# Conditions of the modulation in PSUM, half of the modulated tiles by rows on TensorE, and the first norm's roots in banks of their own

## The chip, the cores and the metric

The kernel runs on one core of one Trainium2 chip. The metric is the device time of one execution in microseconds (us). The engines are named as in the profile: PE (TensorE, matrix products), DVE (VectorE), ACT (ScalarE), POOL (GpSimd) and SP (SyncE, which issues the loads named here).

## The reference

Two layers work on a stream `x` of 1024 latent tokens by 1024 channels. Both are modulated by a conditioning vector `c`; the 256 context tokens `ctx` of the even layer are modulated by another one, `c_ctx`:

```python
sc, scc = silu(c), silu(c_ctx)
shift, scale, gate = split(sc @ mod_w[l] + mod_b[l], 3)       # 1024 -> 3 x 1024
hx = rmsnorm(x, norm_g[l]) * (1 + scale) + shift
shift_c, scale_c, _ = split(scc @ mod_w[l] + mod_b[l], 3)     # even layer only
hc = rmsnorm(ctx, norm_g[l]) * (1 + scale_c) + shift_c
```

The even layer projects `hx` and `hc` (`va, vg, ga, xb, gb`), runs a convolution branch and a bidirectional recurrence, and projects back. The odd layer projects, pools over windows, mixes inside groups with `w_grp`, gates and projects back. The whole runs in float32.

## The kernel before, in words

Channels lie on the 128 partitions and tokens along the free dimension, so `x` is eight tiles `x_0..x_7` of 128x1024 (`KT` = 8). Wide products are made of three matmuls on split operands (high by high, high by low, low by high); `split` lets ACT cast the high half (L95) and another engine subtract the low half (L96).

The change lies in the first stage, which ends with the first matmul of `project_xb(0)` (L125). Four kinds of work run side by side there:

- **The first norm of x.** ACT squares each `x` tile; POOL adds up the squares of the left half of the tokens, DVE those of the right half (L290). `rstd_cols` turns each sum into reciprocal roots: four small matmuls add over the partitions (L187), ACT takes the root (L188), DVE the reciprocal (L189) and a diagonal tile `dg_x` (L191), and one more matmul (L194; an fp32 matmul, which the trace shows as two passes) spreads the roots over all partitions. Sums and spread roots of one half share one two-bank PSUM tile, `wide(...)`.
- **The modulation vectors of layer 0, in two ways.** `modulation(k)` loads two 128x1024 tiles of `mod_w` (shift and scale of channel tile k) and multiplies each on DVE with `cL` and with `cC`, which are SiLU(c) and SiLU(c_ctx) spread over all partitions, and adds up along the row (L206; output `junk`): four big DVE instructions for each k. `mod_row(j)` does the last `KR` tiles of shift (j = 0) or scale (j = 1) on PE: the two conditions as columns (`ccv`) against pieces of `mod_w` (L313), giving two rows; ACT copies the rows (L316), small matmuls turn them into columns (`modt`, L319), and DVE adds the bias into `m0` (L321). Before, tiles 0 to 5 (`KD` = 6) go by DVE and two by rows.
- **`modulate(k)`** scales `x_k` by the roots and by `a0` (L329, two halves), ACT adds the shift and casts the high half `h0h_k` (L332), and DVE makes the low half `h0l_k` (L333). These are what `project_xb(0)` multiplies.
- **Two of the four folds of the odd layer's weights**, `fold(0)` and `fold(1)`: `w_grp` times `wu` on PE (L243 to L245), 24 matmuls for each of four pieces, with `gh`/`gl` the split group matrix (ACT and DVE, L95 and L96) and `wh_wu`/`wl_wu` the split weights (ACT and POOL). They fill PE in the stage.

The small PSUM tiles (`psum`, tag "mm") come from a pool of four banks, the wide ones from two pairs of banks, "cv" and "xb". The program is built with `schedule_with_timeline_sim=True`: a scheduler sets the order of each engine's instructions from its own estimates when the program is built, and each engine then works its list in that order. `load` puts the loads of the stage behind one another on SP's queue. After the stage, PE goes on with the projections.

Of the kernel before, what the change touches and what calls it, by code (L numbers as in the profile page):

```python
# [9 lines left out]
F32 = mybir.dt.float32  # L10
F32R = mybir.dt.float32r
AF = mybir.ActivationFunctionType
# [3 lines left out]
P = 128  # L16
# [3 lines left out]
D = 1024  # L20
KT = D // P
H = 512
HALF = (slice(0, H), slice(H, S))
# [20 lines left out]
O_FG = O_OS + 2 * KT  # L44
N_SM = O_FG + KT

KD = 6
KR = KT - KD
KW = 4 // ((KR + 1) // 2)

# [5 lines left out]
def body(ctx, tc, xT, ctxT, cc, ccol, modT, modW, win, gw, wout, wu, grp, wg, wo1, small, edge, ident, outT):  # L56
    nc = tc.nc
# [17 lines left out]
    def dtile(name, dt=F32):  # L75
        return dpool.tile([P, S], dt, tag="d", name=name)
# [4 lines left out]
    def ttile(name):  # L81
        return tpool.tile([P, H], F32, tag="t", name=name)

    def atile(name):
        return apool.tile([P, NR * PW], F32, tag="acc", name=name)

    def psum(name):
        return pm.tile([P, H], F32, tag="mm", name=name)


    def wide(name, n):
        return pc.tile([P, S], F32, tag=("cv", "xb")[n % 2], name=name)
# [8 lines left out]
    def load(out, src):  # L101
        with ExitStack() as lctx:
            if chain[0] is not None:
                lctx.enter_context(tc.issue_after(chain[0].ins))
            d = nc.sync.dma_start(out, src)
            if chain[0] is not None:
                chain[0] = d
# [27 lines left out]
    def col(o, n=1):  # L135
        return sm[:, o : o + n]

    ones = base.tile([P, P], F32, name="ones")
# [39 lines left out]
        nc.vector.reciprocal(acc, rt[:, :n])  # L178


    def rstd_cols(acc, name, idD, rpool, wn):
        n = acc.shape[-1]
        nt = n // P
        ps = wide(f"ms_{name}", wn)
        r = rpool.tile([P, H // P], F32, tag="rc", name=f"rc_{name}")[:, :nt]
        for c in range(nt):
            nc.tensor.matmul(ps[:, c : c + 1], acc[:, c * P : (c + 1) * P], ones[:, 0:1], start=True, stop=True)  # L187
        nc.scalar.activation(r, ps[:, :nt], AF.Sqrt, bias=eps_r)  # L188
        nc.vector.reciprocal(r, r)  # L189
        t = ttile(f"dg_{name}")[:, :n]  # L190
        nc.vector.tensor_tensor(out=t.rearrange("p (c t) -> p c t", t=P),  # L191
                                in0=idD.unsqueeze(1).to_broadcast([P, nt, P]),
                                in1=r.unsqueeze(2).to_broadcast([P, nt, P]), op=mult)
        nc.tensor.matmul(ps[:, H : H + n], ones, t, start=True, stop=True)  # L194
        return ps[:, H : H + n]

    m0 = base.tile([P, 2, 3 * KT], F32, name="m0")
# [4 lines left out]
    def mod_tile(t, l, m, raw, vecs, junk):  # L204
        for i, vec in enumerate(vecs):
            nc.vector.scalar_tensor_tensor(out=junk, in0=raw, scalar=1.0, in1=vec,  # L206
                                           op0=mult, op1=mult, accum_out=t[:, i, m : m + 1])
        n = len(vecs)
        v = t[:, :n, m]
        nc.vector.tensor_tensor(out=v, in0=v, in1=col(O_MB + l * 3 * KT + m).to_broadcast([P, n]), op=add)  # L210

    def mod_scale(t, a, l, k):
        n = t.shape[1]
        nc.vector.scalar_tensor_tensor(out=a[:, :, k], in0=t[:, :, KT + k], scalar=1.0,
                                       in1=col(O_NG + l * KT + k).to_broadcast([P, n]), op0=add, op1=mult)
# [38 lines left out]
    cpool = tc.alloc_tile_pool(name="cpool", bufs=1)  # L254
    cth = [cpool.tile([P, D], F32R, name=f"cth{i}") for i in range(2)]
    ctl = [cpool.tile([P, D], F32R, name=f"ctl{i}") for i in range(2)]
    cL = cpool.tile([P, D], F32, name="cL")
    hh, hl, ch, cl = [], [], [], []
    with ExitStack() as sctx:
        fpool = sctx.enter_context(tc.tile_pool(name="fpool", bufs=6))  # L260
        gpool = sctx.enter_context(tc.tile_pool(name="gpool", bufs=4))
        spool = sctx.enter_context(tc.tile_pool(name="spool", bufs=1))
# [9 lines left out]
        def fold_some(n):  # L272
            for _ in range(n):
                next(folds, None)

        cC = spool.tile([P, D], F32, name="cC")
        cx = [spool.tile([P, D], F32, name=f"cx_{i}") for i in range(2)]


# [1 line left out]
        acc = [atile("ssq0"), atile("ssq1")]  # L281
# [12 lines left out]
        def modulation(k):  # L294
            for m in (k, KT + k):
                raw = dtile(f"mod0_{m}")
                load(raw, modT[0, m])
                mod_tile(m0, 0, m, raw, (cL, cC), junk)
            mod_scale(m0, a0, 0, k)
# [3 lines left out]
        idx = spool.tile([P, P], F32, name="idx")  # L303
        ccv = spool.tile([P, KT, 2], F32, name="ccv")

        def mod_row(j):
# [11 lines left out]
            for e in range(KR):  # L318
                nc.tensor.matmul(pst[:, :, e], row[:, e * P : (e + 1) * P], idx[:2, :2], start=True, stop=True)  # L319
            ms = slice(j * KT + KD, (j + 1) * KT)  # L320
            nc.vector.scalar_tensor_tensor(out=m0[:, :, ms], in0=pst, scalar=1.0 / D,  # L321
# [35 lines left out]
        nc.scalar.activation(ccv, ccv, AF.Silu)  # L357
        load(idx, ident)
        for i, t in enumerate((cL, cC)):
            ps = wide(f"c_{i}", i)  # L360
            for h in range(2):
                nc.tensor.matmul(ps[:, HALF[h]], ones[:1], cx[i][:1, HALF[h]], start=True, stop=True)
            nc.scalar.activation(t, ps, AF.Silu, scale=float(D))
        def ctx_load(i):
            load(cx[i].rearrange("p (k n) -> p k n", n=C), ctxT[4 * i : 4 * i + 4].rearrange("k p n -> p k n"))
            for q4 in range(4):
# [23 lines left out]
        modulation(1)  # L390
        x_load(7)
        modulation(2)
        rx = [rstd_cols(acc[h][:, :H], f"x{h}", idx, spool, h) for h in range(2)]
        mod_row(1)
        mod_row(0)
        fold_some(2)
        for k in range(KD, KT):
            mod_scale(m0, a0, 0, k)
        modulation(4)
        fold_some(1)  # L400
        modulate(0)
        modulation(3)
        modulation(5)
        modulate(1)
        modulate(2)
        modulate(3)
# [14 lines left out]
    with ExitStack() as actx:  # L421
# [6 lines left out]
        def ltile(name, dt=F32):  # L428
            return lpool.tile([P, E], dt, tag="l", name=name)

        def recurrence(j, uc, gates):
            rs, ius, ats = gates[0::2], gates[1::2], []
            for d in range(2):
                cd = d * KT + j
                at = ltile(f"a{j}_{d}")
                ats.append(at)
                nc.scalar.activation(at, rs[d], AF.Exp, scale=cneg[:, cd : cd + 1])

                th = nc.scalar.activation(rs[d], rs[d], AF.Tanh, scale=chalf[:, cd : cd + 1])
                nc.gpsimd.tensor_tensor(out=ius[d], in0=ius[d], in1=uc, op=mult)  # L440
            for d in range(2):
                r, iu, at = rs[d], ius[d], ats[d]
                with tc.issue_after(th.ins):
                    nc.scalar.activation(r, r, AF.Sqrt, bias=tiny)  # L444
                nc.gpsimd.tensor_tensor(out=iu, in0=iu, in1=r, op=mult)  # L445
                nc.vector.scalar_tensor_tensor(out=iu, in0=at, scalar=1.0, in1=iu, op0=add, op1=mult)  # L446
                if d == 0:
                    ctx_, lat = slice(0, C), slice(C, E)
                    first = iu[:, C - 1 : C]
                else:  # L450
                    ctx_, lat = slice(C - 1, None, -1), slice(E - 1, C - 1, -1)
                    first = iu[:, 0:1]
                nc.vector.tensor_tensor_scan(out=iu[:, ctx_], data0=at[:, ctx_], data1=iu[:, ctx_],
                                             initial=0.0, op0=mult, op1=add)
                nc.vector.tensor_tensor_scan(out=iu[:, lat], data0=at[:, lat], data1=iu[:, lat],  # L455
                                             initial=first, op0=mult, op1=add)
            hs = ius[0]
            nc.gpsimd.tensor_tensor(out=hs[:, C:], in0=hs[:, C:], in1=ius[1][:, C:], op=add)
            nc.sync.dma_start(yb_raw[j], hs[:, C:])

            m = 2 * KT + j
            raw = ltile(f"mod0_{m}")
            nc.sync.dma_start(raw[:, :D], modT[0, m])
            mod_tile(m0, 0, m, raw[:, :D], (cL,), raw[:, :D])


        state = None
# [11 lines left out]
        for j in range(KT):  # L479
            uc = utile(f"uc{j}")  # L480

            for src, dst in zip(xb, (uc[:, :C], uc[:, C:])):
                n = src.shape[-1]
# [11 lines left out]
            for h in range(2):  # L495
                ps = psum(f"vg{j}_{h}")
                mm3(ps, w, (hh, hl), HALF[h])
                t = ttile(f"sg{j}_{h}")
# [5 lines left out]
            for h in range(2):  # L504
                ps = psum(f"va{j}_{h}")
# [9 lines left out]
            for d in range(2):  # L515
                for gi, ob in ((0, O_BR), (1, O_BI)):
                    kc = slice((2 * gi + d) * P, (2 * gi + d + 1) * P)
                    t = ltile(f"g{j}_{d}_{gi}")
                    for a, n in ((0, C), (C, H), (C + H, H)):
                        ps = psum(f"g{j}_{d}_{gi}_{a}")  # L520
# [139 lines left out]
    for j in range(KT):  # L660
        w = wload(win[4 * KT + j], f"gb{j}", nc.gpsimd)
        th, tl = d2tile(f"ybh{j}", F32R), d2tile(f"ybl{j}", F32R)
        for h in range(2):
            ps = psum(f"gb{j}_{h}")
# [48 lines left out]
    for h in range(2):  # L713
        ps = wide(f"mu{h}", h)[:, :H]
# [15 lines left out]
    for m in range(KT):  # L730
        w = wload(wout[m, 1], f"wob{m}", nc.gpsimd)
        for h in range(2):
            ps = psum(f"wob{m}_{h}")
            mm3(ps, w, (bh, bl), HALF[h])
            t = vtile(f"xp{m}_{h}")
# [36 lines left out]
    for i in range(KH):  # L772
        for j in (i, KH + i):
            w = wload(win[2 * KT + j], f"ga{j}", nc.gpsimd)
            for h in range(2):
                ps = psum(f"ga{j}_{h}")
# [63 lines left out]
    idD = cH[:, :P]  # L840
# [54 lines left out]
    for i in range(KH):  # L895
# [3 lines left out]
        t = block_sums(b11, b12, b21, b22, ttile(f"xt3_{i}"), nc.vector)  # L899
# [105 lines left out]
    for m in range(0, NK, 2):  # L1005
# [38 lines left out]
        elif m <= KT:  # L1044
            n = 2 * KT + m - 2
            for q in range(2):
                raw = dtile(f"mod1_{n + q}")
# [183 lines left out]
    m = KT - 4  # L1231
# [56 lines left out]
def layout(i):  # L1288
# [43 lines left out]
    for g, w in enumerate(WINDOWS):  # L1332
        for t in range(w // 2):
            edge[g, t] = w / (t + w // 2)
        for q in range(w // 2 - 1):
# [8 lines left out]
        "modT": f(mw.transpose(0, 2, 1).reshape(2, 3 * KT, P, D)),  # L1344
        "modW": f(mw[0].reshape(KT // KW, KW, P, 3, D)[:, :, :, :2, KD * P :].transpose(3, 0, 2, 1, 4)
                  .reshape(2, KT // KW, P, KW * KR * P)),
# [27 lines left out]
```

## Time and profile before

| | us |
|---|---|
| runs | 1391.06, 1392.81, 1392.95; median 1392.81 |
| profiled execution, time | 1389.0 |
| profiled execution, span of the instructions | 1387.1 |
| busy: PE / DVE / ACT / POOL | 1297.7 / 1172.6 / 655.7 / 401.7 |

The profiled execution is 3.8 us below the median of the runs, and 1.9 us of its time lie around the span. The mean granted PE clock is 0.972 of full speed. PE is busy 94% of the span and DVE 85%, but the shares are means over stages; the first stage is some 92 us of the 1387.1, and its rows decide what a change in it is worth.

### The profile page before, as it was taken

The numbers are of one execution on the slowest core, as the hardware profiler recorded it, in microseconds if no ns is written. First come the engines' busy times: TensorE is split into PE (matmuls) and PEld (weight loads), VectorE is DVE, ScalarE is ACT, GpSimd is POOL, SyncE is SP. The second block draws the span as 40 slices with busy tenths as digits, with TensorE's granted clock in tenths as the row PEclk, the third lists the DMA queues.
The fourth block names the chain that finished last, engine by engine and source line by source line (L and its number), as shares of the span: only waits on it lengthen the run. The fifth ranks groups of instructions, "written<-read, shape, count | busy, mean of one in ns | idle before, by whom it ended". The sixth has DMA issues, their size and how long they took to land.

```text
span 1387.1 us, 15661 instructions
## 1 busy us (share of the span) xinstructions
PE 1297.7 (94%) x5664; PEld 1051.2 (76%) x5664; DVE 1172.6 (85%) x1563; ACT 655.7 (47%) x928; POOL 401.7 (29%) x198
## 2 busy tenths in 40 slices
PE   7889989997998798999999899999999999999896
PEld 4468777786777686888888788778888888777685
DVE  7984898799888989999678874999999986886775
ACT  6352754763764672412633544754333334633442
POOL 5173626745645664542521004100000000000002
PEclk9999999999999999999999999999999999999998
DMA  9741111111211122344254636523334324757623
GB/s 352 279 137 39 38 61 53 65 58 62 68 38 69 61 76 99 107 144 151 99 188 156 212 121 205 155 88 130 134 132 144 115 94 150 253 197 266 217 107 121
DMA packets 82865, 181.79 MB, mean 131 GB/s; under 512 B 7778, under 2 KB 27618, under 8 KB 82788
## 3 DMA queue, kind: packets, MB, share of 16 engines
q1 hardware_dynamic: 74340, 176.60, 37.3%
q10 hardware_dynamic: 8448, 4.20, 1.0%
q8 instruction: 44, 0.72, 0.2%
q14 instruction: 33, 0.27, 0.1%
HBM read 136.72 MB, written 44.04 MB: 130 GB/s over the span
## 4 chain that ended last, share of the span: by engine, by line
PE 57%; DVE 24%; ACT 6%; issue 5%; DMA 4%; POOL 3%; SPq 0%; POOLq 0%; DVEq 0%; ACTq 0%
DVE conv L688 6%; DVE g L455 2%; PE wob L126 2%; PE wob L125 2%; PE wob L127 2%; PE ga L125 2%; PE ga L126 2%; PE ga L127 2%; DVE junk L206 1%; PE fold L245 1%; PE fold L244 1%; PE fold L243 1%; DVE ws L928 1%; DVE mod L206 1%; PE vg L125 1%
## 5 line engine op out<-in xcount | busy, mean ns | idle before, releaser
L688 DVE SCALAR_TENSOR_TENSOR conv<-u,sm,conv 128x1009 f32<-128x1009 f32 (+14 forms) x240 | 301.1, 1274 | 21.6 <-ACT conv L681 18.4
L1194 POOL TENSOR_TENSOR o<-x,rr 128x256 f32<-128x256 f32 (+1 forms) x9 | 8.0, 925 | 459.1 <-ACT rr L1182 456.2
L96 POOL TENSOR_TENSOR wl_wu<-wr_wu,wh_wu 128x1024 fp32r<-128x1024 f32 x16 | 38.7, 2421 | 153.1 <-ACT wh_wu L95 147.4
L521 PE MATMUL g<-uh,wh_gw 128*128 128x512 f32 (+1 forms) x96 | 40.9, 426 | 27.8 <-ACT g L524 16.7
L524 ACT ACTIVATE g<-g,sm 128x512 f32<-128x512 f32 (+1 forms) x96 | 54.0, 622 | 18.8 <-PE g L523 12.2
L125 PE MATMUL gb<-h0h,wh_gb 128*128 128x512 f32 x128 | 51.7, 404 | 5.6 <-ACT sb L669 5.6
L243 PE MATMUL fold<-gh,wh_wu 128*128 128x512 f32 x128 | 52.6, 412 | 4.6 <-ACT wh_wu L95 4.6
L244 PE MATMUL fold<-gl,wh_wu 128*128 128x512 f32 x128 | 51.7, 404 | 3.7 <-DVE gl L96 3.7
L446 DVE SCALAR_TENSOR_TENSOR g<-a,g 128x1280 f32<-128x1280 f32 x16 | 36.4, 2273 | 20.6 <-POOL g L445 20.6
L245 PE MATMUL fold<-gh,wl_wu 128*128 128x512 f32 x128 | 51.2, 409 | 2.7 <-POOL wl_wu L96 2.7
L445 POOL TENSOR_TENSOR g<-g,g 128x1280 f32<-128x1280 f32 x16 | 50.6, 3180 | 9.8 <-ACT g L444 9.8
L440 POOL TENSOR_TENSOR g<-g,uc 128x1280 f32<-128x1280 f32 x16 | 47.3, 2956 | 21.1 <-ACT g L524 19.4
L126 PE MATMUL gb<-h0l,wh_gb 128*128 128x512 f32 x128 | 51.4, 402 | 0.0
L127 PE MATMUL va<-h0h,wl_va 128*128 128x512 f32 x128 | 49.6, 391 | 2.0 <-POOL wl_va L96 2.0
L95 ACT CAST wq_wo<-wr_wo 128x512 fp32r<-128x512 f32 x48 | 28.8, 619 | 47.4 <-DMA wr_wo<-wo 13.8
L127 PE MATMUL gb<-h0h,wl_gb 128*128 128x512 f32 x128 | 51.1, 400 | 0.0
L126 PE MATMUL wob<-ybl,wh_wob 128*128 128x512 f32 x128 | 50.3, 394 | 0.0
L127 PE MATMUL ga<-h0h,wl_ga 128*128 128x512 f32 x128 | 50.2, 392 | 0.0
L127 PE MATMUL wob<-ybh,wl_wob 128*128 128x512 f32 x128 | 50.0, 393 | 0.0
L125 PE MATMUL xb<-h0h,wh_xb 128*128 128x512 f32 x128 | 49.9, 390 | 0.0
L125 PE MATMUL wob<-ybh,wh_wob 128*128 128x512 f32 x128 | 49.9, 394 | 0.0
L126 PE MATMUL xb<-h0l,wh_xb 128*128 128x512 f32 x128 | 49.9, 390 | 0.0
(549 smaller groups left out, 4360.4 us busy)
## 6 DMA issues: line engine op xcount, KB each, us to landing
mod<-modT SPq DMA_DIRECT2D x28, 512.0 KB, 3.8
wr_wu<-wu SPq DMA_DIRECT2D x16, 512.0 KB, 4.1
x_part<-xp SPq DMA_DIRECT2D x32, 256.0 KB, 3.4
mod<-modT SPq DMA_DIRECT2D x32, 256.0 KB, 3.2
wr_v<-wfold SPq DMA_DIRECT2D x16, 512.0 KB, 4.1
wr_g<-wg SPq DMA_DIRECT2D x16, 512.0 KB, 4.2
wr_wo<-wo SPq DMA_DIRECT2D x16, 512.0 KB, 4.3
yr_t<-y_t SPq DMA_DIRECT2D x16, 512.0 KB, 5.5
```

Source lines behind the costliest of these rows:

```text
L96: eng.tensor_tensor(out=lo, in0=src, in1=hi.bitcast(F32), op=sub))
L125: nc.tensor.matmul(ps, hi[:, kc], xh[k][:, cols], start=(k == 0), stop=False)
L126: nc.tensor.matmul(ps, hi[:, kc], xl[k][:, cols], start=False, stop=False)
L127: nc.tensor.matmul(ps, lo[:, kc], xh[k][:, cols], start=False, stop=(k == ks - 1))
L243: nc.tensor.matmul(ps, wh[:, kc], gh[i], start=(i == 0), stop=False)
L244: nc.tensor.matmul(ps, wh[:, kc], gl[i], start=False, stop=False)
L245: nc.tensor.matmul(ps, wl[:, kc], gh[i], start=False, stop=(i == 3))
L440: nc.gpsimd.tensor_tensor(out=ius[d], in0=ius[d], in1=uc, op=mult)
L445: nc.gpsimd.tensor_tensor(out=iu, in0=iu, in1=r, op=mult)
L521: nc.tensor.matmul(ps[:, :n], gwh[:, kc], uh[:, a : a + n], start=True, stop=False)
L524: nc.scalar.activation(t[:, a : a + n], ps[:, :n], AF.Sigmoid, bias=col(ob + d * KT + j))
L688: nc.vector.scalar_tensor_tensor(out=acp[:, a:b], in0=us[j][:, a + o : b + o], scalar=col(O_CONVW + 31 * j + k), in1=acp[:, a:b], op0=mult ...
```

## The change

1. `KD` goes from 6 to 4. Tiles 4 and 5 leave `modulation` and join 6 and 7 in `mod_row`; the eight L206 instructions of `modulation(4)` and `modulation(5)` go. Each `mod_row` still makes eight fp32 matmuls, now 512 columns wide instead of 256, from four loads of 512 KB instead of two, and turns four tiles into columns instead of two. The sum of bytes is the same: sixteen tiles of 512 KB.
2. `cL` and `cC` are no longer SBUF tiles. The product that spreads them stays in its wide PSUM tile, SiLU works in place, and L206 reads the PSUM tile. For the gates, which are made later in the recurrence, ACT copies `cL` to an SBUF tile `cS`.
3. The wide pairs are thus taken, and `rstd_cols` of x uses two "mm" banks for each half, `ms_x` for the sums and `root_x` for the spread roots. The two roots hold two of the four banks until `x_7` is scaled.

```diff
-KD = 6
+KD = 4
...
-    def rstd_cols(acc, name, idD, rpool, wn):
+    def rstd_cols(acc, name, idD, rpool, wn=None):
...
-        ps = wide(f"ms_{name}", wn)
+        if wn is None:
+            ps, root = psum(f"ms_{name}"), psum(f"root_{name}")
+        else:
+            ps = wide(f"ms_{name}", wn)
+            root = ps[:, H : H + n]
...
-        nc.tensor.matmul(ps[:, H : H + n], ones, t, start=True, stop=True)
-        return ps[:, H : H + n]
+        nc.tensor.matmul(root, ones, t, start=True, stop=True)
+        return root
...
-    cL = cpool.tile([P, D], F32, name="cL")
+    cS = cpool.tile([P, D], F32, name="cS")
...
-        cC = spool.tile([P, D], F32, name="cC")
+        cL, cC = wide("cL", 0), wide("cC", 1)
...
-            ps = wide(f"c_{i}", i)
             for h in range(2):
-                nc.tensor.matmul(ps[:, HALF[h]], ones[:1], cx[i][:1, HALF[h]], start=True, stop=True)
-            nc.scalar.activation(t, ps, AF.Silu, scale=float(D))
+                nc.tensor.matmul(t[:, HALF[h]], ones[:1], cx[i][:1, HALF[h]], start=True, stop=True)
+            nc.scalar.activation(t, t, AF.Silu, scale=float(D))
+        nc.scalar.copy(cS, cL)
...
-        rx = [rstd_cols(acc[h][:, :H], f"x{h}", idx, spool, h) for h in range(2)]
+        rx = [rstd_cols(acc[h][:, :H], f"x{h}", idx, spool) for h in range(2)]
...
-        modulation(4)
         fold_some(1)
         modulate(0)
         modulation(3)
-        modulation(5)
...
-            mod_tile(m0, 0, m, raw[:, :D], (cL,), raw[:, :D])
+            mod_tile(m0, 0, m, raw[:, :D], (cS,), raw[:, :D])
```

The scheduler orders the instructions anew. In the rows below a line number, the operation, and output and inputs stand; a trailing number of a tile only tells one use from another. First PE before, from the sums of the first norm to the first matmul of `fold(0)`'s last piece:

```order
L187 MATMUL ms_x0_422<-ones_119,ssq0_184 128x1 x4
L187 MATMUL ms_x1_433<-ones_119,ssq1_185 128x1 x4
L313 MATMUL modr_1_444<-modw_1_0_445,ccv_189 2x256 x4
L194 MATMUL ms_x0_422<-dg_x0_430,ones_119 128x512
L313 MATMUL modr_1_444<-modw_1_1_451,ccv_189 2x256 x4
L194 MATMUL ms_x1_433<-dg_x1_441,ones_119 128x512
L319 MATMUL modt_1_459<-idx_188,modrow_1_457 128x2 x2
...
L319 MATMUL modt_0_478<-idx_188,modrow_0_476 128x2 x2
L243 MATMUL fold_0_3_0_488<-gh_0_0_205,wh_wu_0_3_484 128x512
```

Here `modr_1` is cut in two and lies between the small products of the norm, and `modr_0` follows `modt_1`.

And PE after, at the same place (line numbers are 4 higher there):

```order
L191 MATMUL ms_x0_422<-ones_119,ssq0_185 128x1 x4
L198 MATMUL root_x0_423<-dg_x0_431,ones_119 128x512
L191 MATMUL ms_x1_434<-ones_119,ssq1_186 128x1 x4
L198 MATMUL root_x1_435<-dg_x1_443,ones_119 128x512
L317 MATMUL modr_1_446<-modw_1_0_447,ccv_190 2x512 x2
...
L317 MATMUL modr_1_446<-modw_1_3_459,ccv_190 2x512 x2
L323 MATMUL modt_1_465<-idx_189,modrow_1_463 128x2 x4
L317 MATMUL modr_0_471<-modw_0_0_472,ccv_190 2x512 x2
...
L317 MATMUL modr_0_471<-modw_0_3_484,ccv_190 2x512 x2
L323 MATMUL modt_0_490<-idx_189,modrow_0_488 128x2 x4
L247 MATMUL fold_0_3_0_502<-gh_0_0_205,wh_wu_0_3_498 128x512
```

Now all four products of the norm come first, and both `mod_row`s follow, ahead of the fold.

DVE before, from the bias of the last rows (`modt_0`) to the low halves `gl_1_0` and `gl_1_1` of the second fold's group matrix, on which nearly all of `fold(1)` rests:

```order
L321 SCALAR_TENSOR_TENSOR m0_160<-modt_0_478,sm_115 128x2x2
L333 SCALAR_TENSOR_TENSOR h0l_2_620<-x_2_276,m0_160,h0h_2_619 128x1024
L210 TENSOR_TENSOR m0_160<-m0_160,sm_115 128x2
L206 SCALAR_TENSOR_TENSOR junk_187,m0_160<-mod0_12_539,cL_171 128x1024
L206 SCALAR_TENSOR_TENSOR junk_187,m0_160<-mod0_12_539,cC_181 128x1024
L96 TENSOR_TENSOR gl_1_0_523<-graw_1_0_520,gh_1_0_522 128x1024
...
L96 TENSOR_TENSOR gl_1_1_529<-graw_1_1_526,gh_1_1_528 128x1024
```

The low half `gl_1_0` comes four instructions after the bias of the last rows (one of them two columns wide).

DVE after, the same stretch and the few instructions ahead of it:

```order
L210 SCALAR_TENSOR_TENSOR junk_188,m0_160<-mod0_11_599,cC_182 128x1024
L214 TENSOR_TENSOR m0_160<-m0_160,sm_115 128x2
L218 SCALAR_TENSOR_TENSOR a0_161<-m0_160,sm_115 128x2
L325 SCALAR_TENSOR_TENSOR m0_160<-modt_0_490,sm_115 128x2x4
L333 SCALAR_TENSOR_TENSOR x_3_284<-x_3_284,a0_161,root_x0_423 128x512
...
L333 SCALAR_TENSOR_TENSOR x_7_403<-x_7_403,a0_161,root_x1_435 128x512
L337 SCALAR_TENSOR_TENSOR h0l_3_620<-x_3_284,m0_160,h0h_3_619 128x1024
L337 SCALAR_TENSOR_TENSOR h0l_4_626<-x_4_368,m0_160,h0h_4_625 128x1024
L96 TENSOR_TENSOR gl_1_0_537<-graw_1_0_534,gh_1_0_536 128x1024
L337 SCALAR_TENSOR_TENSOR h0l_5_632<-x_5_376,m0_160,h0h_5_631 128x1024
L96 TENSOR_TENSOR gl_1_1_543<-graw_1_1_540,gh_1_1_542 128x1024
```

Between the instruction that takes `modt_0` from PE and `gl_1_0` there stood one `h0l` and two L206; now ten scalings of `x_3` to `x_7` (five tiles, two halves) and two `h0l` stand there, and `gl_1_1` follows one `h0l` later.

## Prediction

> **What bounds the kernel now.** I read first the busy time in stretches of the first stage, then the chain that ended last, then the engines' own rows. In the stretches the columns are the busy us (and instructions) of PE, PE's weight load, DVE, ACT and POOL, then the granted PE clock, the DMA share and GB/s:
>
> ```profile
> core 0: us, PE busy (x) PEld busy (x) DVE busy (x) ACT busy (x) POOL busy (x), PEclk, DMA share, GB/s
> 26.00:53.00 27.00, 23.68 (x102) 14.13 (x102) 26.49 (x41) 12.19 (x20) 12.09 (x7) 0.94 1.02 385
> 53.00:92.00 39.00, 30.66 (x122) 23.55 (x122) 38.79 (x52) 20.35 (x31) 21.54 (x12) 0.96 0.50 155
> 92.00:143.00 51.00, 51.00 (x250) 43.10 (x249) 26.56 (x26) 14.81 (x17) 22.01 (x16) 1.00 0.17 54
> ```
>
> Until 92 us DVE has hardly a gap (65.28 of 66 us), and PE idles 11.7 us; from 92 us on it is PE that has none, 51.00 of 51.00. So whatever moves PE's start at 92 moves the work behind it by as much, and whatever leaves that start alone brings nothing there. The chain of work that ended last says who sets that start (start, us, engine, tile, line):
>
> ```profile
> 57.85 1.19 DVE h0l L333
> 59.12 1.16 DVE junk L206 x2
> 61.53 1.15 DVE gl L96
> 84.91 2.39 POOL wl_wu L96
> ```
>
> It runs along DVE's queue to `gl_1_0`, which ends at 62.7, and goes over to PE's fold. PE's own rows show the same from the other side (start, duration, line, tiles, shape; in brackets the idle time before and who ended it):
>
> ```profile
> 58.39 0.61 PE L243 MATMUL fold<-gh,wh_wu 128*128 128x512 f32 x2
> 62.72 0.50 PE L244 MATMUL fold<-gl,wh_wu 128*128 128x512 f32 x1 [3.71 <-DVE gl L96]
> 67.16 0.39 PE L244 MATMUL fold<-gl,wh_wu 128*128 128x512 f32 x1
> 67.39 0.39 PE L245 MATMUL fold<-gh,wl_wu 128*128 128x512 f32 x1
> 70.10 0.50 PE L243 MATMUL fold<-gh,wh_wu 128*128 128x512 f32 x1 [0.48 <-ACT wh_wu L95]
> 72.55 0.50 PE L245 MATMUL fold<-gh,wl_wu 128*128 128x512 f32 x1 [1.25 <-POOL wl_wu L96]
> 85.00 0.70 PE L175 MATMUL ms_c<-ssqc,ones 128*128 128x256 f32 x2 [2.16 <-POOL ssqc L290]
> 87.34 0.50 PE L245 MATMUL fold<-gh,wl_wu 128*128 128x512 f32 x1 [0.72 <-POOL wl_wu L96]
> 92.03 0.39 PE L125 MATMUL xb<-h0h,wh_xb 128*128 128x512 f32 x1
> ```
>
> PE waits 3.71 us for `gl_1_0`, then needs 29.31 us to the first `xb` matmul. Of these 4.6 are waits (0.48 + 1.25 + 2.16 + 0.72). In step a fold matmul costs 0.23 (67.16 to 67.39); right after the long wait twelve of them take 4.44 (62.72 to 67.16) in place of 2.7, so a restart costs 1.7. Hence the question: when does `gl_1_0` end in the changed kernel, and what does PE then still have to do?
>
> **The change, part by part.** *Conditions in PSUM.* Rows of DVE with L206, and one small addition, in the part where POOL works too:
>
> ```profile
> 17.05 2.18 DVE L206 SCALAR_TENSOR_TENSOR junk<-mod,cC 128x1024 f32<-128x1024 f32 x1
> 19.27 1.12 DVE L210 TENSOR_TENSOR m<-m,sm 128x2 f32<-128x2 f32 x1
> 30.79 2.33 DVE L206 SCALAR_TENSOR_TENSOR junk<-mod,cL 128x1024 f32<-128x1024 f32 x1
> 34.74 2.30 DVE L206 SCALAR_TENSOR_TENSOR junk<-mod,cC 128x1024 f32<-128x1024 f32 x1
> 37.08 0.16 DVE L210 TENSOR_TENSOR m<-m,sm 128x2 f32<-128x2 f32 x1
> 37.16 1.22 DVE L206 SCALAR_TENSOR_TENSOR junk<-mod,cL 128x1024 f32<-128x1024 f32 x1
> ```
>
> Once POOL is done, L206 takes 1.22; beside POOL 2.18 to 2.33, and the addition 1.12 instead of 0.16. What a PSUM input does is seen where both kinds stand beside the same sort of POOL instruction:
>
> ```profile
> 47.94 2.72 DVE L329 SCALAR_TENSOR_TENSOR x<-x,a,ms_x 128x512 f32<-128x512 f32 x4
> 54.32 3.45 DVE L206 SCALAR_TENSOR_TENSOR junk<-mod,cC 128x1024 f32<-128x1024 f32 x1
> 47.96 2.37 POOL L96 TENSOR_TENSOR wl_wu<-wr_wu,wh_wu 128x1024 fp32r<-128x1024 f32 x1 [12.00 <-ACT wh_wu L95]
> 54.29 2.40 POOL L96 TENSOR_TENSOR wl_wu<-wr_wu,wh_wu 128x1024 fp32r<-128x1024 f32 x1 [3.96 <-ACT wh_wu L95]
> ```
>
> L329, with one input in PSUM, goes through a POOL subtraction of 2.37 at 0.68 for each half tile; L206, with both inputs in SBUF, stands still for the whole of one of 2.40 (3.45 - 1.2 = 2.2). So L206 reading PSUM should take 1.22 beside POOL: 1.11 (30.79) and 1.08 (34.74) come off at once. Another 0.96 (17.05) and 0.96 (19.27) come off earlier, and reach later rows only as far as ACT's squares, which DVE waits for in between, move up with them. I take all four, a lead of 4.1 us at the roots; the ends are 2.2 (the first two alone) and, an estimate, 5.0 (POOL's own additions, on which the first root waits, are no longer held up by L206 either).
>
> A rule of the Trainium skill speaks against this part: "VectorE: DVE Perf Modes", section "Rules for kernel authors", advises, for elementwise work on a matmul's output, to copy it to SBUF first if many operations read it; here sixteen L206 will. This row has the price of reading PSUM:
>
> ```profile
> L487 DVE SCALAR_TENSOR_TENSOR uc<-xb,sm,uc 128x1023 f32<-128x1023 f32 x4 | 5.1, 1282 | 0.1
> ```
>
> It is 1.28 for 1023 elements against 1.22 from SBUF, 1.0 us for sixteen, some of it in DVE's idle time later. By the rule the copy of before should win, the lead would be a loss of up to 1.0, and the sum below would be 5 us longer. The rows beside POOL say otherwise, and I go by them, without the 1.0.
>
> The copy `cS` costs ACT 1.0 (the SiLU beside it takes as long):
>
> ```profile
> 10.93 1.02 ACT L363 ACTIVATE cC<-c 128x1024 f32<-128x1024 f32 x1 [0.83 <-PE c L362]
> ```
>
> 0.83 us of idle time cover most of it; nothing in the sum.
>
> *Roots and rows on PE.* The rows now:
>
> ```profile
> 39.14 1.25 PE L187 MATMUL ms_x<-ones,ssq 128*128 128x1 f32 x8 [2.07 <-DVE ssq L290]
> 40.31 3.30 PE L313 MATMUL modr<-modw,ccv 128*2 128x256 f32 x8
> 43.54 1.12 PE L194 MATMUL ms_x<-dg_x,ones 128*128 128x512 f32 x2
> 44.60 1.89 PE L313 MATMUL modr<-modw,ccv 128*2 128x256 f32 x8
> 47.62 0.60 PE L319 MATMUL modt<-idx,modrow 2*128 2x2 f32 x4
> 48.15 3.62 PE L313 MATMUL modr<-modw,ccv 128*2 128x256 f32 x16
> 52.27 0.60 PE L319 MATMUL modt<-idx,modrow 2*128 2x2 f32 x4 [0.51 <-ACT modrow L316]
> 42.67 0.69 DVE L191 TENSOR_TENSOR dg_x<-idx,rc_x 128x512 f32<-128x512 f32 x1
> 46.43 1.40 DVE L329 SCALAR_TENSOR_TENSOR x<-x,a,ms_x 128x512 f32<-128x512 f32 x2
> ```
>
> Now half of `modr_1` and more lies in gaps in which PE waits for DVE's diagonals, and all rows are out at 51.8. In the new order both roots come first, and no row is in the gaps. Step by step: the first diagonal ends at 43.36 - 4.1 = 39.3 and its root is spread 1.1 later. Before the second diagonal DVE has two L206 (2.4), two scalings (1.4), four small ones (0.3) and the diagonal itself (0.7): 44.0 (sum with gaps, 4.7). Its root is out at 45.1. Only then come the rows: 32 passes of 512 columns. A pass of 256 takes 3.62 / 16 = 0.226; one of 512 I take as twice that, 0.453, together 14.5. The bounds are 0.23 (if columns cost nothing) and 0.56 (half of L194's 1.12). Each `mod_row` then has ACT's copy (0.5 of waiting) and eight `modt` passes in place of four (2 x 0.6): 1.7, or 3.5 for both. After a pause like that before 40.31 the first eight passes cost 3.30 against 1.89; I put half of these 1.4 in. `modt_0` is out at 45.1 + 14.5 + 3.5 + 0.7 = 63.8, where it now is at 52.9.
>
> *DVE behind `modt_0`.* The eight L206 that go (8 x 1.22 = 9.8 us, 12.0 with the stall at 54.32) lay in DVE's queue ahead of `gl_1_0`. But `gl_1_0` now stands behind the bias of `modt_0`, so DVE first waits for PE, and then does ten scalings (2.72 / 4 = 0.68 each, overlapped 0.66: 6.6), two `h0l` (2.4), and `gl_1_0` (1.15), 0.15 for the bias: 10.3. A POOL subtraction of 2.4 may fall on one of the last three; I put 1.2. `gl_1_0` ends at 63.8 + 10.3 + 1.2 = 75.3 against 62.7.
>
> *PE behind `gl_1_0`.* `fold(1)` has 96 matmuls, of which four need no `gl` and come first: 92 x 0.23 = 21, the restart 1.7, the sum for the context 0.35 (half of 85.00's, as the fold beside it overlaps): 23. The 4.6 of waits I take as gone, since the casts and context squares behind them are not tied to `gl_1_0` and have 12 us more. So `xb` starts at 98.3 against 92.0: **6.3 us later**.
>
> *The rest.* Bytes are as before, and requests of 512 KB at 385 GB/s take 1.4 each: the four more pieces that now lie before the last `modw` land at most 5.5 later, while the last rows run 12 later. The two banks that the roots hold are free again at the tenth scaling, before `gl_1_0`, for which the pieces that want them wait anyway; if that cover fails, it is a wait inside the same 75.3. From 92 to 143 PE is full, so the 6.3 stay.
>
> The sum: 1389.0 + 6.3 = 1395.3 for an execution like the profiled one; the runs' median lies 3.8 above that, so 1392.8 + 6.3 = **1399.1**.
>
> **The rivals.** (a) *Columns cost little in these passes* (other sign). If an fp32 pass with only two columns of weights is bound by something per pass, 32 passes take 7.2 instead of 14.5; `modt_0` is out at 56.5, and with the lead at 5.0 and no POOL stall, `xb` starts at 98.3 - 7.2 - 0.9 - 1.2 = 89.0, 3.0 earlier: 1389.8. The point from which it gains, with the same lead and no stall, is 6.3 - 0.9 - 1.2 = 4.2 off the passes: 10.3 for all, 0.32 each. For it: no row shows these passes at 512. Against: L194's passes of 512 take 0.56 each, two and a half times L313's of 256. (b) *The waits come back and passes are slow*: 0.56 each (+3.4), the full cold start (+0.7), and half of PE's 4.6 us of waits again (+2.3): 12.7 later, 1405.5. For it: the context's squares and `wl_wu` on POOL set PE's pace at 85.00 and 87.34 now. (c) *PSUM inputs do not free L206 from POOL*, the change does not do what it says: no lead, +4.1, 10.4 later, 1403.2; L329 at 47.94 speaks against it. (The rule of the Trainium skill's page "VectorE: DVE Perf Modes" would end here or up to 1.0 later.) (d) *The delay is given back*: PE's later stages have slack that the first stage does not show, 1392.8 and so no change; 51.00 of 51.00 speaks against it, PE's 57% of the chain for it in part:
>
> ```profile
> PE 57%; DVE 24%; ACT 6%; issue 5%; DMA 4%; POOL 3%; SPq 0%; POOLq 0%; DVEq 0%; ACTq 0%
> ```
>
> **How the numbers follow.** Forecast 0.68 (its own range by the lead's, the start's and the stall's ends: 4 to 9 later), (a) 0.08, (b) 0.10, (c) 0.06, (d) 0.08. A measurement of this kernel tells 0.2%, about 2.8 us, from no change. Slower by more: forecast, (b) and (c) without a small tail, 0.82; within: (d) and a part of (a) and of the tail, 0.10; faster: the rest of (a), 0.08. The range leaves out (a) and (d), 0.16: from 1395.0 (a little over 2 later) to 1406.0, so that (b) is in.
>
> **What would show it.** In the changed profile: L206 near 1.2 beside POOL (step one; 2.2 or more means (c)); the second root near 45 and `modr` after it, 0.45 a pass (0.23 means (a), 0.56 (b)); `modt_0` near 63 to 64; PE's wait for `gl_1_0` longer than 3.71, about 5, ending near 75; the first `xb` matmul near 98, and the same 6 us still there at 143. The prediction is wrong if `gl_1_0` ends before 66, or if PE has gaps between 98 and 149 that before did not have.

## The result and the profile after

The changed kernel takes 1398.6 us (median of seven runs, 1394.56 to 1400.37) against 1391.06 of before on the same chip (seven runs, 1388.76 to 1396.66). The ratio is 1.0047, with a 95% interval of 1.0028 to 1.0066: slower by some 6.5 us (the two medians lie 7.5 apart; the ratio is taken over all runs). The forecast was 1399.1 in a range of 1395.0 to 1406.0. The profiled execution took 1398.34 us, its span is 1396.6.

The busy time by stretches, after (columns as shown for before):

```profile
26.00:53.00 27.00, 21.75 (x71) 11.46 (x69) 23.06 (x39) 10.40 (x15) 9.61 (x6) 0.81 1.01 381
53.00:92.00 39.00, 32.54 (x121) 21.28 (x122) 26.38 (x35) 18.39 (x28) 15.28 (x12) 0.91 0.36 105
92.00:143.00 51.00, 50.27 (x245) 42.36 (x244) 13.55 (x16) 15.97 (x19) 23.67 (x16) 1.00 0.30 91
```

DVE, which was full until 92 us, now has 26.38 of 39 us: the removed work is gone, and the time with it isn't. What PE did in those stretches (start, duration, line, tiles; lines are higher by 4):

```profile
33.64 0.95 PE L191 MATMUL ms_x<-ones,ssq 128*128 128x1 f32 x8
38.32 2.05 PE L198 MATMUL root_x<-dg_x,ones 128*128 128x512 f32 x2 [3.73 <-DVE m L214]
40.16 1.71 PE L191 MATMUL ms_x<-ones,ssq 128*128 128x1 f32 x8
43.31 2.04 PE L198 MATMUL root_x<-dg_x,ones 128*128 128x512 f32 x2 [1.45 <-DVE dg_x L195]
45.29 7.65 PE L317 MATMUL modr<-modw,ccv 128*2 128x512 f32 x16
53.65 1.05 PE L323 MATMUL modt<-idx,modrow 2*128 2x2 f32 x8 [0.72 <-ACT modrow L320]
54.63 7.03 PE L317 MATMUL modr<-modw,ccv 128*2 128x512 f32 x16
62.38 1.05 PE L323 MATMUL modt<-idx,modrow 2*128 2x2 f32 x8 [0.72 <-ACT modrow L320]
...
75.91 0.79 PE L248 MATMUL fold<-gl,wh_wu 128*128 128x512 f32 x1 [4.10 <-DVE gl L96]
...
99.66 0.39 PE L125 MATMUL xb<-h0h,wh_xb 128*128 128x512 f32 x1
101.12 0.50 PE L127 MATMUL xb<-h0h,wl_xb 128*128 128x512 f32 x1 [0.72 <-POOL wl_xb L96]
```

Both roots first, then both sets of rows with hardly a gap, then the transposed `modt_0` out at 63.43 (52.27 + 0.60 = 52.87 before), the wait for `gl_1_0`, and `xb` at 99.66 in place of 92.03. DVE's rows between `modt_0` and `gl_1_0`, and its idle time later:

```profile
63.46 0.17 DVE L325 SCALAR_TENSOR_TENSOR m<-modt,sm 128x8 f32<-128x8 f32 x1 [0.88 <-PE modt L323]
63.55 6.68 DVE L333 SCALAR_TENSOR_TENSOR x<-x,a,root_x 128x512 f32<-128x512 f32 x10
70.14 4.58 DVE L337 SCALAR_TENSOR_TENSOR h0l<-x,m,h0h 128x1024 fp32r<-128x1024 f32 x2
74.65 1.21 DVE L96 TENSOR_TENSOR gl<-graw,gh 128x1024 fp32r<-128x1024 f32 x1
...
90.38 1.75 DVE L178 RECIPROCAL ssqc<-sq_c 128x256 f32<-128x256 f32 x1 [9.80 <-ACT sq_c L177]
```

The chain that ended last goes the same way, in order of time:

```profile
45.36 7.59 PE modr L317 x16
...
54.70 6.97 PE modr L317 x16
...
66.85 2.12 DVE x L333 x4
...
74.65 1.22 DVE gl L96
...
94.94 3.77 POOL cx L344 x7
```

### The profile page after: what moved, and what is told of

It is laid out like the page before. It is cut to its first block, busy times and chain, and to the rows that moved or that the text cites. A ratio compares the mean times of both kernels' runs of the same rounds, so it can differ in the third digit from the quotient of the medians.

```text
span 1396.6 us, 15662 instructions
## 1 busy us (share of the span) xinstructions
PE 1304.8 (93%) x5672; PEld 1049.5 (75%) x5672; DVE 1150.6 (82%) x1543; ACT 656.2 (47%) x929; POOL 394.0 (28%) x198
## 4 chain that ended last, share of the span: by engine, by line
PE 39%; DVE 33%; DMA 11%; ACT 7%; issue 6%; POOL 3%; SPq 0%; POOLq 0%; DVEq 0%; ACTq 0%
DVE conv L690 10%; DVE g L457 2%; PE ga L127 2%; PE ga L126 2%; PE ga L125 2%; DVE ws L930 2%; DMA wr_g<-wg 2%; DMA yr_t<-y_t 2%; DVE mod L210 2%; DMA wr_v<-wfold 1%; PE fold L248 1%; PE fold L249 1%; PE fold L247 1%; DVE g L448 1%; DVE g L455 1%
## 5 line engine op out<-in xcount | busy, mean ns | idle before, releaser
L127 PE MATMUL xb<-h0h,wl_xb 128*128 128x512 f32 x128 | 50.3, 393 | 0.7 <-POOL wl_xb L96 0.7
```

The lines of the kernel that those rows point to most:

```text
L127: nc.tensor.matmul(ps, lo[:, kc], xh[k][:, cols], start=False, stop=(k == ks - 1))
```

## The experiments

Whole runs of this kernel differ by several us. So each variant is given twice: by its ratio to before, and by the start of the first convolution instruction on DVE in its profile. That row comes shortly after the stage and stands in every kernel:

```profile
129.86 1.27 DVE L688 SCALAR_TENSOR_TENSOR conv<-u,sm,conv 128x1009 f32<-128x1009 f32 x1 [1.28 <-ACT conv L681]
138.46 1.27 DVE L690 SCALAR_TENSOR_TENSOR conv<-u,sm,conv 128x1009 f32<-128x1009 f32 x1 [1.28 <-ACT conv L683]
```

By this mark the changed kernel is 8.6 us late. Each mark comes from one profiled execution, and no run shows how far it scatters, so differences of less than a microsecond say little. All eight combinations of the three parts were measured; "pair" is the wide PSUM pair of before, "two banks" the change's separate banks for sums and roots, and "shared" one small bank for both, which stands for the pair where the conditions in PSUM take the pairs. (With the conditions in SBUF and KD = 4 both were run; their marks are 0.7 us apart.)

| variant | KD | conditions | sums and roots | first convolution, against 129.86 | ratio to before (95%) |
|---|---|---|---|---|---|
| before | 6 | SBUF | pair | 0 | 1 |
| rows only | 4 | SBUF | pair | +2.5 | 1.0052 (1.0032 to 1.0071) |
| roots only | 6 | SBUF | two banks | +8.0 | 1.0057 (1.0034 to 1.0080) |
| rows and roots | 4 | SBUF | two banks | +13.8 | 1.0094 (1.0075 to 1.0114) |
| PSUM and roots | 6 | PSUM | two banks | -3.1 | 0.9988 (0.9970 to 1.0006) |
| the change | 4 | PSUM | two banks | +8.6 | 1.0047 (1.0028 to 1.0066) |
| PSUM, shared | 6 | PSUM | shared | -9.3 | 0.9934 (0.9915 to 0.9953) |
| PSUM and rows, shared | 4 | PSUM | shared | -3.7 | 0.9947 (0.9930 to 0.9964) |

My theory at the start of the experiments ("banks"): the two more banks that the first norm takes put all rows behind both roots, and that order is what costs the time. The main rival ("rows"): the doubled passes cost it, wherever they stand.

**Only the roots in banks of their own.** The edit, on before:

```diff
+        ps, root = psum(f"ms_{name}"), psum(f"root_{name}")
...
-        nc.tensor.matmul(ps[:, H : H + n], ones, t, start=True, stop=True)
+        nc.tensor.matmul(root, ones, t, start=True, stop=True)
```

> Only the roots in banks of their own: KD = 6, conditions in SBUF. Theory banks: no lead, and all rows stand behind the second root, which comes out near 50 (5 us later than in the changed kernel's 45.3): +5 to +9 us. Theory rows, and theory PSUM reads: nothing that costs is in it, -1 to +1 us.

It took 1398.24 us (median of 7) against 1391.47. PE's rows:

```profile
43.22 2.04 PE L198 MATMUL root_x<-dg_x,ones 128*128 128x512 f32 x2 [6.05 <-DVE m L214]
48.21 2.05 PE L198 MATMUL root_x<-dg_x,ones 128*128 128x512 f32 x2 [1.45 <-DVE dg_x L195]
50.19 4.22 PE L317 MATMUL modr<-modw,ccv 128*2 128x256 f32 x16
```

PE stands still 6.05 us for the first diagonal, where it did half of `modr_1` before, and the rows start at 50.19 instead of 40.31. So two banks alone cost as much as the whole change. The rivals expected nothing here and fall as the only cause.

**The change with a shared bank.** One edit on the changed kernel; the root product overwrites the sums, which ACT has read:

```diff
-            ps, root = psum(f"ms_{name}"), psum(f"root_{name}")
+            ps = root = psum(f"ms_{name}")
```

> The changed kernel with one bank for the sums and the spread roots of each half (the root product overwrites the sums, which ACT has read by then), so two of the four small banks are free for the rows. Everything else as changed: KD = 4, conditions in PSUM. Theory banks: modr_1 lies between the products again, gl_1_0 no longer stands behind the ten scalings: 9 to 13 us faster than the changed kernel, 3 to 7 us faster than before. Theory rows: as the changed kernel, +5 to +8 us against before.

1383.16 us (median of 6), ratio 0.9947: 0.5% below before, where the change is 0.5% above. PE again:

```profile
33.48 1.84 PE L191 MATMUL ms_x<-ones,ssq 128*128 128x1 f32 x16
35.24 1.88 PE L317 MATMUL modr<-modw,ccv 128*2 128x512 f32 x4
38.15 1.10 PE L198 MATMUL ms_x<-dg_x,ones 128*128 128x512 f32 x2 [1.02 <-DVE m L214]
39.17 5.31 PE L317 MATMUL modr<-modw,ccv 128*2 128x512 f32 x12
44.42 1.12 PE L198 MATMUL ms_x<-dg_x,ones 128*128 128x512 f32 x2
...
54.20 1.05 PE L323 MATMUL modt<-idx,modrow 2*128 2x2 f32 x8 [0.72 <-ACT modrow L320]
```

The first set of rows fills the gaps around the first diagonal, and `modt_0` is out at 55.25, 8.2 us earlier than in the change. On DVE, `gl_1_0` starts 4.7 us behind the instruction that takes `modt_0` (11.2 in the change), since the built order no longer has the ten scalings ahead of it:

```profile
55.76 0.15 DVE L325 SCALAR_TENSOR_TENSOR m<-modt,sm 128x8 f32<-128x8 f32 x1
60.45 1.23 DVE L96 TENSOR_TENSOR gl<-graw,gh 128x1024 fp32r<-128x1024 f32 x1 [0.80 <-ACT gh L95]
```

At the mark that is 12.3 us (138.46 to 126.20). That the order follows from how many banks are free when the program is built is inferred: in every variant with two banks both roots come before all rows, and in every variant with the pair or the shared bank rows lie between them. The overwriting alone does not explain it, since the pair has that order too and overwrites nothing. How the scheduler weighs the banks stays open.

PE stood still longer there, and it was also granted less clock. From 36 to 47 us its granted clock (third column from the end) was 0.84 in before, 0.53 in the changed kernel and 1.00 with the shared bank:

```profile
36.00:47.00 11.00, 8.81 (x35) 4.20 (x36) 10.93 (x25) 2.54 (x6) 0.00 (x0) 0.84 1.05 391
36.00:47.00 11.00, 7.23 (x15) 3.26 (x16) 9.18 (x22) 1.08 (x2) 0.00 (x0) 0.53 1.04 402
36.00:47.00 11.00, 9.98 (x29) 2.75 (x28) 8.71 (x22) 1.48 (x3) 0.00 (x0) 1.00 1.04 401
```

There a spread of roots takes 2.05 and 2.04 in the changed kernel and 1.10 and 1.12 with the shared bank. So the order costs in two ways, by the standing and by slower products; no run separates the two.

**The conditions in PSUM, roots in two banks, KD = 6.** The changed kernel with `KD = 6` and `modulation(4)` and `(5)` back.

> Conditions in PSUM and roots in banks of their own, KD = 6 as before. Theory banks: the first diagonal stays 5 us early as in the changed kernel (37.5 in place of 42.7), the rows stand behind both roots but are short (7 us instead of 14.7 in all), gl_1_0 comes 1 to 4 us earlier than before: -4 to 0 us. Theory rows: nothing is left but the lead, -5 us. A third theory, that reading PSUM costs DVE the time: +5 us or more.

1389.36 us (median of 12), ratio 0.9988: no difference that is clear of the scatter, and 3.1 us early at the mark. Against "roots only", from which it differs in the place of the conditions alone, it is 11.1 us early. The theory that PSUM reads cost time falls. One step of the theory "banks" was wrong here: `gl_1_0` does not come 1 to 4 us earlier than before. It ends at 63.19, 0.5 later.

```profile
56.77 0.15 DVE L325 SCALAR_TENSOR_TENSOR m<-modt,sm 128x4 f32<-128x4 f32 x1
61.97 1.22 DVE L96 TENSOR_TENSOR gl<-graw,gh 128x1024 fp32r<-128x1024 f32 x1
63.24 0.50 PE L248 MATMUL fold<-gl,wh_wu 128*128 128x512 f32 x1 [0.30 <-DVE gl L96]
```

The gain lies behind it: from there PE needs 25.6 us to `xb` (63.24 to 88.87) instead of 29.31, and the granted clock from 53 to 92 us was 1.00 instead of 0.96.

**Rows and roots, conditions in SBUF.** The change without its PSUM part (`cL`, `cC` as SBUF tiles, no `cS`).

> KD = 4 and roots in banks of their own, but the conditions in SBUF: the change without its PSUM part. If the parts add up along one chain (no lead, second root near 48, then 14.7 us of rows, then the ten scalings ahead of gl_1_0): +12 to +18 us against before, so that PSUM is worth 6 to 10 us inside the change. Rival (the later of two waits decides, so that rows or roots alone already cost all): +7 to +9 us, and PSUM is worth nothing there.

1405.19 us (median of 6), +13.8 at the mark. The rival falls: 13.8 is even more than the 2.5 of the rows alone and the 8.0 of the roots alone together. By the mark the conditions in PSUM are worth 5.2 us inside the change (143.66 to 138.46), a little less than the 6 to 10 expected:

```profile
143.66 1.27 DVE L690 SCALAR_TENSOR_TENSOR conv<-u,sm,conv 128x1009 f32<-128x1009 f32 x1 [1.28 <-ACT conv L683]
```

**Conditions in PSUM with a shared bank, KD = 6.**

> Conditions in PSUM, one bank for sums and roots of a half, KD = 6: the change without the longer rows and without the two more banks. Theory banks: the lead of 5 us at the first diagonal stays, the rows lie between the products of the norm again, modt_0 is out near 48 (52.9 before): the first stage ends 5 to 9 us earlier than before, and so does the whole if the later order stays. Rival (PSUM helps only where DVE waits for PE anyway): as the variant with PSUM and separate banks, -3 to 0 us.

1382.67 us (median of 6), 9.3 us early at the mark, where the theory had 5 to 9. With this corner the change can be summed in steps: PSUM -9.3, rows +5.6 (to 126.20), two banks +12.3, together +8.6. These sizes hold for this sequence of steps alone. With KD = 6 the two banks cost 6.2 (-9.3 to -3.1), and the rows that come after them 11.7 (-3.1 to +8.6): some 6 us arise only where rows and banks meet. `gl_1_0` shows where. With KD = 6 and two banks it starts 5.2 us behind the instruction that takes `modt_0` (56.77 to 61.97 above), with KD = 4 and two banks 11.2, behind the ten scalings.

**KD = 4 alone: a miss.** On before, `KD = 4`, without `modulation(4)` and `(5)`.

> Only KD = 4: conditions in SBUF, sums and roots in one wide pair, as before. Theory banks (the four small banks that the first norm takes keep the rows behind both roots; that order costs the time): the first mod_row goes back between the products of the norm, half of its doubled passes in gaps of PE, and 9.8 us of L206 leave DVE: time as before, -2 to +2 us. Theory rows (the doubled passes cost it wherever they stand, 0.44 us each for 32): at least as much as the whole change, +6 to +10 us.

1399.22 us (median of 6), 7.2 over before by the ratio: by the whole time the rival's number. But the mark is only 2.5 late, and the rest comes at 598 us, in the output projection of the recurrence's branch:

```profile
598.13 0.50 PE L125 MATMUL wob<-ybh,wh_wob 128*128 128x512 f32 x1 [4.36 <-ACT ybh L95]
```

Before has no such wait there. The built order of that place had changed too (DVE's products `yr` and ACT's casts `ybh` stand at other places among the convolution's instructions), though no code of it had. Whether the rows or that later order cost the time, the next run had to tell.

**KD = 4 with a shared bank, conditions in SBUF.** The built order of that later place is again that of before.

> KD = 4 with the conditions in SBUF and one small bank for sums and roots of a half. The variant with KD = 4 alone lost 7.2 us, of which only 2.5 were there at the first convolution instruction and 4.5 came in at 598 us, where PE waits for ybh and the built order differs from before; here the built order of that later place is the one of before. Theory later order: the first convolution comes 0 to 3 us later than before and the whole is -3 to +3 us. Rival (the doubled rows cost it all, the jump at 598 us is only how it shows): +6 to +8 us.

1390.71 us (median of 12), ratio 0.9992 (0.9971 to 1.0013), with 1.8 us at the mark:

```profile
131.61 1.27 DVE L690 SCALAR_TENSOR_TENSOR conv<-u,sm,conv 128x1009 f32<-128x1009 f32 x1 [1.28 <-ACT conv L683]
```

So with the conditions in SBUF the rows as such cost 2 us where they lie between the products of the norm (5.6 with the conditions in PSUM), and the 7.2 of the miss were mostly a new order far behind. The rival falls. By the traces, the order behind the stage differs from that of before in three more variants: between 350 and 450 us in this one and in the change with a shared bank, and between 900 and 1100 us with the conditions in PSUM, a shared bank and KD = 6. For these three the whole time may hold something that is not the stage's, and the mark is the better measure.

**`gl_1_0` off DVE's queue.** The changed kernel with one edit in `fold`:

```diff
-            split(raw, th, tl, nc.vector)
+            split(raw, th, tl, nc.gpsimd if g == 1 else nc.vector)
```

> The changed kernel with the low halves gl_1_0 and gl_1_1 subtracted on POOL instead of DVE, so that they no longer stand behind the ten scalings. Theory DVE queue (the step of the prediction: gl_1_0 comes last behind modt_0 and the scalings, PE waits 4.1 us for it): 2 to 4 us faster than the changed kernel, since POOL needs 2.4 us and ACT's cast of gh_1_0 ends near 69.8. Rival (the wait is covered by others that end as late): no change against the changed kernel, within 1 us.

1393.54 us (median of 12), ratio 1.0023 (1.0005 to 1.0040); 3.6 us less than the change at the mark (134.83). PE's wait of 4.10 is gone, up to the rests that POOL's slower subtraction leaves:

```profile
73.34 0.50 PE L248 MATMUL fold<-gl,wh_wu 128*128 128x512 f32 x1 [0.53 <-POOL gl L96]
80.02 0.50 PE L248 MATMUL fold<-gl,wh_wu 128*128 128x512 f32 x1 [0.76 <-POOL gl L96]
```

So the place of `gl_1_0` behind `modt_0` and the scalings was on the path, as the prediction had it, and worth 3.6 us of the 8.6 (although `modt_0` itself came 1.0 us later there, at 64.43).

**KD = 5, conditions in PSUM, shared bank.** Three tiles by rows of 384 columns, five by DVE.

> Conditions in PSUM, one bank for sums and roots, KD = 5: three tiles by rows of 384 columns, five by DVE. Theory banks and balance: between KD = 4 and KD = 6 neither PE (rows 10.9 us in all) nor DVE (four L206 less than KD = 6) ends late: 7 to 12 us faster than before, the fastest of the variants. Rival (KD = 4 with a shared bank is the best balance): slower than that one by 1 to 4 us.

1379.46 us (median of 6), ratio 0.9921 (0.9896 to 0.9945): the fastest, 11 us below before, and 1.3% below the change by the two ratios. Its mark is 9.6 early. It lies within the scatter of KD = 6 with a shared bank, so the better balance is not clear of it; that both beat before is.

```profile
49.77 0.82 PE L323 MATMUL modt<-idx,modrow 2*128 2x2 f32 x6 [0.61 <-ACT modrow L320]
58.18 0.50 PE L248 MATMUL fold<-gl,wh_wu 128*128 128x512 f32 x1 [1.65 <-DVE gl L96]
```

Between norm and rows there are hardly any gaps left, `modt_0` is out at 50.59, and PE's wait for `gl_1_0` is down to 1.65.

## Why the prediction was right, and where it was not

**The lead.** Taken 4.1, with an estimated upper end of 5.0; measured 5.2, just above that end: the first diagonal ends at 38.17, against 43.36. Rows of DVE with L210 (L206 before) and of POOL in the changed kernel, and as the last one POOL's of before:

```profile
17.07 1.22 DVE L210 SCALAR_TENSOR_TENSOR junk<-mod,cC 128x1024 f32<-128x1024 f32 x1
37.48 0.69 DVE L195 TENSOR_TENSOR dg_x<-idx,rc_x 128x512 f32<-128x512 f32 x1
15.84 2.65 POOL L294 TENSOR_TENSOR ssq<-ssq,xsq 128x512 f32<-128x512 f32 x2
15.80 4.57 POOL L290 TENSOR_TENSOR ssq<-ssq,xsq 128x512 f32<-128x512 f32 x2
```

L210 takes 1.22 beside POOL's 2.65 us of additions, where it took 2.18 before. POOL gains as well: the same two additions took 4.57 before. This half was missing in the four stalls that I added up, and stood only in the upper end. Rival (c) falls. The Trainium skill ("SBUF — State Buffer", section "Who interferes with whom") states that a VectorE instruction with at most one input in SBUF, outside the two-port modes, does not contend with GpSimd; these rows agree. The page of the Trainium skill that I set against the change ("VectorE: DVE Perf Modes", "Rules for kernel authors") offers, beside reading PSUM as it is, a copy to SBUF where many operations read; sixteen L210 read PSUM here at 1.19 to 1.22, so no price of reading shows, and the copy would bring the stalls back.

**Roots and rows.** Each spread took some 2.04 where I had 1.1, with the granted clock at 0.53 between 36 and 47 us. (With `gl_1_0` on POOL, after the same wait of 3.73 us, the first spread took 1.34, so this size does not follow from the wait alone.) The larger lead made up for it (second root out at 45.35, said 45.1). The 32 passes took 7.65 + 7.03 = 14.7 (said 14.5), so columns do cost, and rival (a) falls. `modt_0` came at 63.43 (said 63.8).

**DVE behind `modt_0`.** 12.4 us to the end of `gl_1_0` instead of 11.5: a POOL subtraction fell on the two `h0l` (4.58 in place of 2.4), where I had put half of one. PE waited 4.10 for it (said about 5). One reading of the prediction is wrong, though the sum does not use it: not all of the eight L206 that go lay ahead of `gl_1_0`. Sixteen L206 stand ahead of it before and sixteen L210 after; four of `modulation(4)` went, and four of `modulation(3)` moved up. So ahead of `gl_1_0` the change took no such work off DVE.

**PE behind `gl_1_0`.** 23.75 us to `xb` (said 23), and none of the 4.6 us of waits came back, so rival (b) falls. `xb` began 7.6 late, 1.3 more than in my sum. One step was left out behind it: the context now comes later, and on POOL its eight L344 stand ahead of the low half of `xb`'s weights, so that PE waits another 0.72 at 101.12:

```profile
93.50 5.22 POOL L344 TENSOR_SCALAR cx<-cx,a,m 128x256 f32<-128x256 f32 x8 [1.65 <-DVE cx L377]
98.68 2.38 POOL L96 TENSOR_TENSOR wl_xb<-wr_xb,wh_xb 128x1024 fp32r<-128x1024 f32 x1
```

**"From 92 to 143 PE is full, so it stays."** PE's only new gap there is the 0.72 at 101.12. By the prediction's own sign (a gap between 98 and 149 that before did not have) this is a miss, if a small one, and the delay behind it is 8.6 us instead of 6.3. Further on the delay moves between 6 and 10 us and is 7.1 at 540 us in the profiles. Then some 2.4 us come back at a pause of PE that ends near 549 before and near 555 after: it is shorter (4.13 instead of 5.64 us), and so is the slow start behind it. Why it is shorter stays open; only here does rival (d) hold. The delay grows again behind it, to 6.7 at 870 us, 8.4 at 1125 us and 9.5 at the end of the two spans (1387.1 and 1396.6). How much of this belongs to the change, and how much to the scatter of single executions, stays open too: the profiled execution of before is 2.1 us below the median of its runs here. So it is in part luck that the sum came so near: it has 6.3 for the start of `xb`, where 7.6 were measured (8.6 at the mark), and the ratio of the whole times makes 6.5. Besides, the 1399.1 was counted from 1392.8, and before took 1391.06 in this comparison.

**The step that failed** is the sentence that the two banks cost nothing, because they are free before the pieces that want them. It asks only for waits in the running kernel, and PE's waits from 60 to 80 us are indeed for `gl_1_0` and for ACT's copies and casts. What it leaves out is that the banks decide the built order. I costed that order step by step and so met the time, without asking where it came from. In the sequence conditions, rows, banks the runs put -9.3, +5.6 and +12.3 us on the three; in the sequence conditions, banks, rows they put -9.3, +6.2 and +11.7.

## What to carry to other kernels

A bank of PSUM that is held a little longer can cost as much as the rest of a change brings (6 to 12 us here, against 5 to 11 for the conditions in PSUM): count what the free banks let an engine do between two waits, and let a result overwrite what has been read. Where a scheduler sets the order, compare the built orders of the whole program, far behind the edit too, before a difference is put down to the edit. And to judge a change in one stage, use a mark at the end of that stage beside the whole time.

## What the hardware showed that I had not expected

A POOL instruction is held up by DVE as well: two additions on POOL took 4.57 us beside L206 with both inputs in SBUF, and 2.65 when one was in PSUM. And the smallest DVE instructions are held up like the large ones. Of these four of 128x2 the first takes 2.04 us and ends with the subtraction on POOL (56.98 and 56.96); the three behind it take 0.15 each:

```profile
54.94 2.25 DVE L218 SCALAR_TENSOR_TENSOR a<-m,sm 128x2 f32<-128x2 f32 x4
54.62 2.34 POOL L96 TENSOR_TENSOR wl_wu<-wr_wu,wh_wu 128x1024 fp32r<-128x1024 f32 x1 [1.38 <-ACT wh_wu L95]
```
